# A hybrid encoder block on one core: projection r by token halves, with half of the features resident

## The chip, the cores and the metric

The kernel runs on one core of one Trainium2 chip. The metric is the device time of one execution in microseconds (us); it is given as the median of several runs. Engines are named as in the profile: PE (TensorE), DVE (VectorE), ACT (ScalarE), POOL (GpSimd) and SP (SyncE, from whose queue nearly all DMAs are issued).

## The reference

One layer, 1024 tokens of width 1024, all float32:

```
h = rmsnorm(x, norm_mix)
q, k, v, r, lr_f, lr_b, u, g_a, g_b = split(h @ w_in)      # 512,512,1024,1024,16,16,512,1024,1024
log_a = log_sigmoid(lr @ w_decay_up + b_decay) / 16        # forward and backward
o = gla_chunked(q, k, v, log_a_f, include_diag=True)       # 4 heads, keys 128, values 256
  + flip(gla_chunked(flip(q), flip(k), flip(v), flip(log_a_b), include_diag=False))
o = rmsnorm_per_head(o) * gla_norm * silu(r);  y_a = o @ w_branch_gla
y_b = (centred mean over windows 2/4/8/16 of u, minus u) @ w_pool_group * pool_scale
x = x + (sigmoid(g_a) * y_a + sigmoid(g_b) * y_b) @ w_out
gate, up = split(rmsnorm(x, norm_ffn) @ w_ffn_in);  x = x + (silu(gate) * up) @ w_ffn_out   # D_FF 2816
out = rmsnorm(x, norm_final)
```

## The kernel before

Every large matrix is split into a high and a low part (a cast on ACT, then a difference on POOL or DVE: `split_to`), and a product is three matmuls (`products`). Most of the large products are done by a Strassen scheme with seven block products p = 1 to 7, so sums of blocks are made on DVE and POOL beside the matmuls.

The order of the work is written out by hand; each engine runs its own queue in the order in which the program emits it, and the DMAs stand in SP's queue. What stands beside the matmuls is emitted by `pump(dt)`, which runs after each three matmuls (`mm3`) with dt = 1 for 512 columns. It keeps four lists:

- `put_off`: steps given by `soon(delay, step)`, first in, first out; `settle` empties the list.
- `pending`: splits of a weight set that `prepare` (called by `take`) has put there. The first comes out after 4 units, the second after 6, since `prepare` sets the credit to -2 and a split needs 2.
- `aside`: one generator of preparatory jobs (`prepare_beside`, `beside`). It counts down in every unit, but runs, at most one job a unit, only while `pending` is empty. `finish_beside` emits all that is left at once.
- `side`: generators begun by `begin`; each yields the units until its next step.

The stages, in order:

1. Norms, features `hT` (8 pairs of slots: pair kp and token half, each as `hh` and `hl`), values of head 0.
2. Low-rank decays, then `project_qk`: q and k of head 0 (four passes of 8 units, each a `feature_major`). Beside it `feature_jobs` makes the sums of features (`hs`) and their splits (`trh`, `trl`). The second half of feature pairs 0 and 1 is written to DRAM (`h_out`) and its slots are freed.
3. Gates: 16 units of Strassen products (u, q, k, v, the merge gates a and b). `Ahead.step` prepares unit weights four steps ahead (`wh`, `wl` from `fs` or `fraw`). `decays` runs as side work, and `pooling` after it. v is transposed and split by `Gates.turn`, which `finish_late` runs after the next product. In the last unit head 0 (`load_head`), the features' second half (`load_features`) and values are loaded.
4. r and attention: eight column tiles of r, for each both token halves with one weight set. `attention(h)` of the four heads runs as side work: a backward scan (7 steps), scores, a forward scan (8 steps) and a normalization, with `SCORES` and `STEP` units between steps. `load_head(h + 1)` and `load_values` fetch the next head. `gated` transposes a finished head and multiplies it by silu(r); `put_by` calls it at the end of each pass. Beside it run the sums of the branch and output weights (`branch_jobs`, `output_jobs`: tile `wsum`, written to `s_out` and `t_wo`), eight blocks of one load and four POOL operations, a job every 2 units.
5. Branch and output projections (`project`): 28 pieces of 8 units. `line_load`, `line_sums` and `line_make` prepare the pieces ahead of their use (`wraw`, `wh`, `wl`, and data as `dh`, `dl`); the tiles `wh` and `wl` have six buffers each, two for a piece.
6. FFN in and out, final norm.

All working tiles come from one pool of 39 slots of 4 KB a partition; a load whose slot isn't free waits in SP's queue. `take()` hands out a prepared weight set and calls `prepare` for the next, whose DMA is issued there.

Of the kernel before, what the change touches and what calls it, by code (L numbers as in the profile page):

```python
# [17 lines left out]
P = 128  # L18
# [33 lines left out]
def kernel(  # L52
# [159 lines left out]
    class Weights:  # L212
# [194 lines left out]
    qk_out = [[dram.tile([P, 2, HALF], F32, name=f"qk_out{h}{n}") for n in range(2)] for h in range(HEADS)]  # L407
    h_out = [[dram.tile([P, 2, HALF], F32, name=f"h_out{kp}{n}") for n in range(2)] for kp in range(2)]
    dec_out = [
# [201 lines left out]
    def decays():  # L611

        for h in range(HEADS):
            for half in (1, 0):
# [55 lines left out]
    def project_qk(amid):  # L670
        qk = [slot(s=s) for s in "qk"]
        for dst, scale in zip(qk, (DK**-0.5, 1.0)):
            w = take(dst is qk[0])
            for half in range(2):
                amid(dst is qk[1], half)
                ps = feature_major(w, hT, half)
                nc.scalar.activation(dst[:, half, :], ps[:, :], AF.Copy, scale=scale)
        for n, t in enumerate(qk):
            later(qk_out[0][n], t[:, :, :])

    def load_head(h):
        q, k = (slot(s=s) for s in "qk")
        qe, ke = {}, {}
        for t, src in ((k, qk_out[h][1]), (q, qk_out[h][0])):
            nc.sync.dma_start(t[:, :, :], src)
        for half in (1, 0):
            for n, (e, s) in enumerate(((qe, "qe"), (ke, "ke"))):
                e[half] = slot(s=s)
                nc.sync.dma_start(e[half][:, :, :], dec_out[h][half][n])
        heads[h] = q, k, qe, ke  # L690

# [11 lines left out]
    def apply_decay(h, half, d):  # L703
        q, k, qe, ke = heads[h]
        for eng, e, x_ in ((nc.vector, ke, k), (nc.gpsimd, qe, q)):
            eng.tensor_tensor(e[half][:, d, :], e[half][:, d, :], x_[:, half, :], op=ALU.mult)

# [3 lines left out]
    def attention(h):  # L711

        q, k, qe, ke = heads[h]

# [45 lines left out]
        if h == 0:  # L760
            for run in RUNS:
                apply_decay(0, *run)
                yield 1.5
            kt_of[0] = transposed_keys(0, 1, 1)
            yield 2
# [3 lines left out]
        for n in range(NT - 1, 0, -1):  # L769
# [9 lines left out]
            if n == 2:  # L779
                kts[0, 0] = transposed_keys(h, 0, 0)  # L780
                yield 0.5
        p = scores(0)
        yield SCORES
        o = [slot(shape=(4, DV), s="o") for _ in range(2)]
        ms = vec(NT, "oms")
        old = sf = None
        for n in range(NT):
            half, i = n // 4, n % 4
            op = bank(ps_g, "op")
            products(op[:, :DV], tokens(p, n), value(n), last=False)  # L790
            terms = []
            if n < NT - 1:
                terms.append((chunk_of(qe, n, 1), sb[half][:, i, :]))
            if n > 0:
                terms.append((chunk_of(qe, n, 0), sf[:, :]))
            for j, (a, b) in enumerate(terms):
                if j == len(terms) - 1 and n < NT - 1:
                    state, old = advance(old, n, 0, kts[half, 0])
                    sf = s1((DV,), "sf")
                    nc.scalar.activation(sf[:, :], state, AF.Copy, scale=factor(n + 1, 0, "before"))  # L800
                nc.tensor.matmul(op[:, :DV], a, b, start=False, stop=j == len(terms) - 1)  # L801
# [32 lines left out]

    STEP = 1.2

    def transposed_keys(h, half, d):
        ke = heads[h][3]
        kp = bank(ps_g, "kp")
# [123 lines left out]
    for half in range(2):  # L963
# [9 lines left out]
        nc.vector.tensor_tensor(lrT[64:96, half, :], ps[64:96, :], as_f32(lrT[64:96, half, :]), op=ALU.subtract)  # L973
    def first_unit(k, half):
        if k:
            gates_ahead.step()

    project_qk(first_unit)
    finish_beside()
# [47 lines left out]
    def line_make():  # L1027
        n = len(made)
        if n < len(line) and not (n // 2 == 1 and len(ob.get((1, 0), ())) <= n % 2):
# [53 lines left out]
    def branch_piece(p, c):  # L1083
# [10 lines left out]
        def make(raw):  # L1094
            b = {1: ob[0, 0], 2: ob[1, 0], 3: ob[1, 1], 4: ob[1, 0], 5: ob[0, 0], 6: t2s, 7: ob[0, 1]}[p][c]
            right = data_split(b)
# [92 lines left out]
    class Gates:  # L1189
# [12 lines left out]
        def run(self, p):  # L1202
# [71 lines left out]
    for n, run in enumerate(gate_runs):  # L1274
# [8 lines left out]
        for at, (of, p) in enumerate(run):  # L1283
# [33 lines left out]
    def project(base, products, collect, before, amid=None, first=FIRST, up=UP, pools_of=lambda p: U_BANKS if p == 1 else X_BANKS):  # L1317
        banks = {}
        for at, p in enumerate(products):
# [4 lines left out]
            for c in range(2):  # L1324
# [75 lines left out]
    def gated(j, half, sr):  # L1400

        tp = bank(ps_g, "tp")
        for i in range(4):
            nc.tensor.transpose(
                tp[:, i * P : (i + 1) * P],
                o_heads[j // 2][half][:, i, (j % 2) * P : (j % 2 + 1) * P], ident[:, :],
            )
        if j // 2 not in oT:
            oT[j // 2] = [slot(s="o") for _ in range(2)], []
        tiles, there = oT[j // 2]  # L1410
        nc.vector.scalar_tensor_tensor(
            tiles[half][:, j % 2, :], tp[:, :], g_gla[:, j : j + 1], sr, op0=ALU.mult, op1=ALU.mult
        )
        there.append((j, half))
        if len(there) == 4:
            c = j // 2 % 2
            for half, t in enumerate(tiles):
                if j < 4:
                    later(ob_out[0, half][:, 2 * c : 2 * c + 2, :], t[:, :, :])
                else:  # L1420
                    ob.setdefault((1, 1 - half), []).append(t)

    def put_by():
        if silu_r and silu_r[0][0] // 2 in o_heads:
            gated(*silu_r.pop(0))

# [8 lines left out]
    prepare_beside(chain(map(branch_jobs, range(4)), map(output_jobs, range(4))), 2)  # L1435
    for j in range(KT):
        w = take()
        r = slot(s="r")
        for half in range(2):
            ps = feature_major(w, hT, half)  # L1440
            flush()
            nc.scalar.activation(r[:, half, :], ps[:, :], AF.Silu)
            silu_r.append((j, half, r[:, half, :]))
# [465 lines left out]
```

## Time and profile before

| | us |
|---|---|
| runs | 1463.4, 1465.99, 1464.22 (median 1464.22) |
| the profiled execution | 1468.01 |
| its span, first to last instruction | 1466.3 |
| PE busy | 1381.7 (94%) |
| DVE busy | 886.8 (60%) |
| POOL busy | 768.9 (52%) |
| ACT busy | 647.4 (44%) |
| mean granted PE clock | 0.979 |

A wait row gives who waited, for what, the sum in us, the number of waits and the longest. A row of a group gives line, engine, operation, output<-inputs, shapes and count; then busy time in us, mean ns of one, and the idle time before them with what ended it. A row in order of time begins with its start and its duration in us; idle time of the engine before it, and what ended that, stands in brackets. SPq rows are DMA issues.

### The profile page before, as it was taken

Reading aid. Unit: us, or ns where it says so; the run is one execution under the profiler, and the core shown is the slowest. Engines: PE = TensorE matmul, PEld = TensorE weight load, DVE = VectorE, ACT = ScalarE, POOL = GpSimd, SP = SyncE. Lnnn points to the kernel's source line nnn. Section 1 sums busy time; section 2 is a strip of 40 time slices with the busy share of each in tenths; the row PEclk is TensorE's granted clock in tenths of the full one; section 3 lists DMA queues with packets and bytes.
Section 4 is the critical chain, followed back from the end, with each engine's and each line's share of the span. In section 5 each row is a group of like instructions: output and inputs, shape, how many; then the busy total and the mean of one; then the engine's idle time right before and its main releaser. Section 6 shows DMA issues by size and latency. Waiting matters only on the chain.

```text
span 1466.3 us, 18225 instructions
## 1 busy us (share of the span) xinstructions
PE 1381.7 (94%) x6365; PEld 1145.0 (78%) x6365; DVE 886.8 (60%) x1103; ACT 647.4 (44%) x1138; POOL 768.9 (52%) x576
## 2 busy tenths in 40 slices
PE   7979988999988989998898999999999999999997
PEld 7858767787877768877776888888888888888876
DVE  6876555687643766766867486555555555543353
ACT  6366765644533333444333643333333334353243
POOL 3244533455635453345764437666666668455354
PEclk9989999999999998999999999999999999999999
DMA  6334535566896786664622535545555556876452
GB/s 212 116 98 132 172 110 197 191 207 209 264 353 236 243 285 223 226 232 155 235 96 101 201 118 177 160 151 163 165 166 165 165 165 231 334 287 232 158 210 77
DMA packets 182588, 279.26 MB, mean 190 GB/s; under 512 B 12088, under 2 KB 102240, under 8 KB 182496
## 3 DMA queue, kind: packets, MB, share of 16 engines
q1 hardware_dynamic: 182496, 278.10, 55.8%
q8 instruction: 50, 0.82, 0.2%
q14 instruction: 42, 0.34, 0.1%
HBM read 182.37 MB, written 95.68 MB: 190 GB/s over the span
## 4 chain that ended last, share of the span: by engine, by line
PE 68%; DVE 9%; issue 7%; DMA 6%; POOL 5%; ACT 4%; SPq 0%; POOLq 0%; DVEq 0%; ACTq 0%
PE ps L269 62%; POOL wl L198 2%; DMA raw<-in_w_in_dram 2%; DMA fraw<-in_w_in_dram 1%; DVE hs L590 1%; DMA pl<-p_out 1%; PE op L801 1%; POOL wsum L590 1%; PE kv L269 1%; DMA hh<-h_out 1%; PE sc L748 1%; ACT wh L197 1%; PE yb L269 1%; DVE fs L866 1%; PE tr L316 1%
## 5 line engine op out<-in xcount | busy, mean ns | idle before, releaser
L198 POOL TENSOR_TENSOR wl<-fs,wh 128x512 fp32r<-128x512 f32 x144 | 198.1, 1378 | 205.6 <-ACT wh L197 173.6
L269 PE MATMUL ps<-gh,wh 128*128 128x512 f32 x616 | 240.6, 391 | 0.0
L269 PE MATMUL ps<-gh,wl 128*128 128x512 f32 x616 | 239.9, 390 | 0.0
L269 PE MATMUL ps<-gl,wh 128*128 128x512 f32 x616 | 239.9, 389 | 0.0
L198 POOL TENSOR_TENSOR wl<-fraw,wh 128x512 fp32r<-128x512 f32 x108 | 155.1, 1436 | 102.6 <-ACT wh L197 98.4
L198 POOL TENSOR_TENSOR ol<-gor,oh 128x1024 fp32r<-128x1024 f32 (+1 forms) x42 | 100.4, 2396 | 93.8 <-ACT oh L197 76.9
L269 PE MATMUL ps<-hh,wh 128*128 128x512 f32 x352 | 147.0, 417 | 0.0
L269 PE MATMUL ps<-hl,wh 128*128 128x512 f32 x352 | 139.3, 396 | 0.0
L269 PE MATMUL ps<-hh,wl 128*128 128x512 f32 x352 | 139.1, 395 | 0.0
L269 PEld LDWEIGHTS ps<-gh,wl 128*128 128x128 f32 x616 | 115.7, 188 | 23.9
L269 PEld LDWEIGHTS ps<-gl,wh 128*128 128x128 f32 x616 | 115.7, 188 | 23.8
L269 PEld LDWEIGHTS ps<-gh,wh 128*128 128x128 f32 x616 | 115.7, 188 | 23.7
L198 POOL TENSOR_TENSOR wl<-wraw,wh 128x512 fp32r<-128x512 f32 x56 | 91.2, 1655 | 75.3 <-ACT wh L197 75.3
L269 PE MATMUL ps<-oh,oh 128*128 128x512 f32 x308 | 120.1, 390 | 2.0 <-DVE x L1831 2.0
L269 PE MATMUL ps<-ol,oh 128*128 128x512 f32 x308 | 120.1, 390 | 0.8 <-DVE ol L198 0.8
L269 PE MATMUL ps<-oh,ol 128*128 128x512 f32 x308 | 119.9, 389 | 0.0
L269 PE MATMUL ps<-trh,wh 128*128 128x512 f32 x256 | 101.7, 397 | 10.6 <-ACT wh L197 8.9
L197 ACT CAST wh<-fs 128x512 fp32r<-128x512 f32 x144 | 88.3, 614 | 29.0 <-DVE fs L866 26.5
L269 PE MATMUL ps<-trh,wl 128*128 128x512 f32 x256 | 100.8, 394 | 0.2 <-POOL wl L198 0.2
L269 PE MATMUL ps<-trl,wh 128*128 128x512 f32 x256 | 100.7, 393 | 0.0
L198 DVE TENSOR_TENSOR ol<-wor,oh 128x1024 fp32r<-128x1024 f32 (+1 forms) x42 | 62.0, 1496 | 52.7 <-ACT oh L197 45.4
L198 POOL TENSOR_TENSOR wl<-raw,wh 128x512 fp32r<-128x512 f32 x23 | 31.4, 1379 | 98.3 <-ACT wh L197 98.3
(254 smaller groups left out, 3063.4 us busy)
## 6 DMA issues: line engine op xcount, KB each, us to landing
fraw<-in_w_ffn_in_dram SPq DMA_DIRECT2D x44, 512.0 KB, 6.0
gor<-g_out SPq DMA_DIRECT2D x35, 512.0 KB, 6.2
fraw<-in_w_in_dram SPq DMA_DIRECT2D x32, 512.0 KB, 6.7
g_out<-s SPq DMA_DIRECT2D x44, 256.0 KB, 2.4
wor<-t_out SPq DMA_DIRECT2D x20, 512.0 KB
g_out<-g SPq DMA_DIRECT2D x33, 256.0 KB, 2.3
x<-in_x_dram SPq DMA_DIRECT2D x16, 512.0 KB, 5.4
wor<-in_w_ffn_out_dram SPq DMA_DIRECT2D x15, 512.0 KB, 11.2
```

Source lines behind the costliest of these rows:

```text
L197: nc.scalar.copy(hi, src)
L198: eng.tensor_tensor(lo, src, as_f32(hi), op=ALU.subtract)
L269: nc.tensor.matmul(ps, a[i], b[j], start=first and n == 0, stop=last and n == 2, skip_group_check=onto)
L316: nc.tensor.transpose(ps[:, c], xt[:, k * P : (k + 1) * P], ident[:, :])
L590: op()
L748: nc.tensor.matmul(sc[d][:, i * CH : (i + 1) * CH], chunk_of(ke, n, d), chunk_of(qe, n, d), start=True, stop=True,)
L801: nc.tensor.matmul(op[:, :DV], a, b, start=False, stop=j == len(terms) - 1)
L866: nc.vector.tensor_tensor(s, a, b, op=op)
```

## The change

The first tile of r (column tile 0, both halves) is computed right after q and k of head 0, and written to `r_out`. The other seven tiles run in stage 4 with the token half as the outer loop, so their weights are loaded and split twice; only the first half of the features stays resident, all four pairs of the second half go to `h_out` and come back during the last two passes of the first half. The first two gate unit steps move from beside k to beside r's tile. `STEP` goes from 1.2 to 0.95, `SCORES` from 6 to 4.5, the pause after each round of decays from 10 to 6. The next head's k, q and values are loaded at other steps. `turn` is given to `soon` with a delay of 5. `finish_beside` in stage 4 stands after tile 5 of the second half, ahead of two more weight sets' use. In `project`, a second `line_make` runs when fewer than n + 3 pieces are made. `gated` keeps its tiles by head and half, and `put_by` takes the first entry whose head is ready.

```diff
-        + [(w_in, KT, R0 + j * P, P) for j in range(KT)]
+        + [(w_in, KT, R0 + j * P, P) for j in (0, *range(1, KT), *range(1, KT))]
...
-    for kp in range(2):
+    for kp in range(4):
         for n, part in enumerate(hT.pair(kp, 1)):
             later(h_out[kp][n], as_f32(part[:, :, :]))
...
-                yield 10
+                yield 6
...
-    SCORES = 6
+    SCORES = 4.5
...
+    def first_r():
+        w = take(False)
+        r = slot(s="r")
+        for half in range(2):
+            gates_ahead.step()
+            ps = feature_major(w, hT, half)
+            nc.scalar.activation(r[:, half, :], ps[:, :], AF.Silu)
+        later(r_out, r[:, :, :])
+
-    def load_features():
-        for kp in range(2):
+    def load_features(kps):
+        for kp in kps:
...
         p = scores(0)
+        if h + 1 < HEADS:
+            load_head(h + 1, "k")
         yield SCORES
...
-                if n == 2:
-                    load_head(h + 1)
+                if n == 1:
+                    load_head(h + 1, "q")
                 if n == 4:
                     load_values(h + 1, 1)
-                if 4 <= n < NT:
-                    apply_decay(h + 1, *RUNS[n - 4])
+                if n == 6:
+                    load_values(h + 1, 0)
+                if 3 <= n < 7:
+                    apply_decay(h + 1, "k", *RUNS[n - 3])
+                if 4 <= n:
+                    apply_decay(h + 1, "q", *RUNS[n - 4])
                 if n == NT - 1:
-                    load_values(h + 1, 0)
                     kt_of[h + 1] = transposed_keys(h + 1, 1, 1)
...
-    STEP = 1.2
+    STEP = 0.95
...
-    project_qk(first_unit)
+    project_qk()
+    first_r()
...
-                late.append(partial(self.turn, int(p == 7)))
+                soon(5, partial(self.turn, int(p == 7)))
...
             if last and at == 1:
                 fetch()
-                load_head(0)
-            elif last and at == 4:
-                load_features()
+                load_head(0, "k")
+            elif last and at == 3:
+                load_head(0, "q")
             elif last and at == 5:
                 prepare()
-            elif last and at == 6:
                 load_values(0, 1)
...
                 line_load()
                 line_make()
+                if len(made) < n + 3:
+                    line_make()
                 line_sums()
...
-    for j in range(KT):
-        w = take()
-        r = slot(s="r")
-        for half in range(2):
+    for half in range(2):
+        for j in range(1, KT):
+            w = take()
+            if j == 1 or j % 2 == 0:
+                r = slot(s="r")
+            if j == 1:
+                nc.sync.dma_start(r[:, 0, :], r_out[:, half, :])
+                silu_r.append((0, half, r[:, 0, :]))
             ps = feature_major(w, hT, half)
             flush()
...
-            if (j, half) == (KT - 2, 1):
+            if half == 0 and j >= KT - 2:
+                load_features((2 * j - 12, 2 * j - 11))
+            elif (j, half) == (KT - 3, 1):
                 finish_beside()
                 line_load()
                 line_load()
+            elif (j, half) == (KT - 2, 1):
                 load_block(0, 0)
+                line_make()
                 load_block(0, 1)
-            elif j == KT - 1:
+            elif (j, half) == (KT - 1, 1):
                 line_make()
```

More of the change, by code (lines that the diff above doesn't have):

```diff
@@ L407 @@
     qk_out = [[dram.tile([P, 2, HALF], F32, name=f"qk_out{h}{n}") for n in range(2)] for h in range(HEADS)]
-    h_out = [[dram.tile([P, 2, HALF], F32, name=f"h_out{kp}{n}") for n in range(2)] for kp in range(2)]
+    h_out = [[dram.tile([P, 2, HALF], F32, name=f"h_out{kp}{n}") for n in range(2)] for kp in range(4)]
+    r_out = dram.tile([P, 2, HALF], F32, name="r_out")
     dec_out = [
@@ L664, in decays, with project_qk @@
                         nc.sync.dma_start(dec_out[h][half][n][:, d, :], t[:, :])
-                yield 10
+                yield 6
     heads, v_heads, o_heads = {}, {}, {}
-    SCORES = 6
-    def project_qk(amid):
+    SCORES = 4.5
+    def project_qk():
         qk = [slot(s=s) for s in "qk"]
         for dst, scale in zip(qk, (DK**-0.5, 1.0)):
-            w = take(dst is qk[0])
+            w = take()
             for half in range(2):
-                amid(dst is qk[1], half)
                 ps = feature_major(w, hT, half)
@@ L679, in project_qk, with load_head @@
             later(qk_out[0][n], t[:, :, :])
[L681 to L685, printed above, removed]
+    def first_r():
[6 more added lines that the diff above has]
+        later(r_out, r[:, :, :])
+    def load_head(h, which):
+        me = heads.setdefault(h, {})
+        n = "qk".index(which)
+        whole = me[which] = slot(s=which)
+        me[which + "e"] = {}
+        nc.sync.dma_start(whole[:, :, :], qk_out[h][n])
         for half in (1, 0):
[L687 to L690, printed above, removed]
+            e = me[which + "e"][half] = slot(s=which + "e")
+            nc.sync.dma_start(e[:, :, :], dec_out[h][half][n])
     def load_values(h, half):
@@ L701, in load_features, with apply_decay @@
                 nc.sync.dma_start(as_f32(t[:, :, :]), h_out[kp][n])
[L703 to L706, printed above, removed]
+    def apply_decay(h, which, half, d):
+        eng = {"q": nc.gpsimd, "k": nc.vector}[which]
+        e = heads[h][which + "e"][half][:, d, :]
+        eng.tensor_tensor(e, e, heads[h][which][:, half, :], op=ALU.mult)
     RUNS = ((1, 1), (0, 1), (0, 0), (1, 0))
@@ L761, in attention @@
             for run in RUNS:
-                apply_decay(0, *run)
+                apply_decay(0, "k", *run)
+                apply_decay(0, "q", *run)
                 yield 1.5
@@ L1028, in line_make @@
         n = len(made)
-        if n < len(line) and not (n // 2 == 1 and len(ob.get((1, 0), ())) <= n % 2):
+        if n < len(line) and (n // 2 != 1 or n % 2 in ob.get((1, 0), ())):
             while len(loads) <= n:
@@ L1400, in gated @@
     def gated(j, half, sr):
+        h, i = j // 2, j % 2
         tp = bank(ps_g, "tp")
[L1403 to L1410, printed above, removed]
+        for t in range(4):
+            nc.tensor.transpose(tp[:, t * P : (t + 1) * P], o_heads[h][half][:, t, i * P : (i + 1) * P], ident[:, :])
+        tile_, there = oT.setdefault((h, half), (slot(s="o"), [])) if (h, half) not in oT else oT[h, half]
         nc.vector.scalar_tensor_tensor(
-            tiles[half][:, j % 2, :], tp[:, :], g_gla[:, j : j + 1], sr, op0=ALU.mult, op1=ALU.mult
+            tile_[:, i, :], tp[:, :], g_gla[:, j : j + 1], sr, op0=ALU.mult, op1=ALU.mult
         )
[L1414 to L1421, printed above, removed]
-    def put_by():
-        if silu_r and silu_r[0][0] // 2 in o_heads:
-            gated(*silu_r.pop(0))
+        there.append(j)
+        if len(there) == 2:
+            if h < 2:
+                later(ob_out[0, half][:, 2 * h : 2 * h + 2, :], tile_[:, :, :])
+            else:
+                ob.setdefault((1, 1 - half), {})[h - 2] = tile_
+    def put_by():
+        for n, (j, half, sr) in enumerate(silu_r):
+            if j // 2 in o_heads:
+                silu_r.pop(n)
+                gated(j, half, sr)
+                return
     def finish_heads():
@@ L1435 @@
     prepare_beside(chain(map(branch_jobs, range(4)), map(output_jobs, range(4))), 2)
[L1436 to L1439 removed]
+    for half in range(2):
+        for j in range(1, KT):
+            w = take()
+            if j == 1 or j % 2 == 0:
[3 more added lines that the diff above has]
+                silu_r.append((0, half, r[:, 0, :]))
             ps = feature_major(w, hT, half)
             flush()
[L1442 to L1443 removed]
+            nc.scalar.activation(r[:, j % 2, :], ps[:, :], AF.Silu)
+            silu_r.append((j, half, r[:, j % 2, :]))
             for _ in range(2):
                 put_by()
[L1446 removed]
+            if half == 0 and j >= KT - 2:
+                load_features((2 * j - 12, 2 * j - 11))
+            elif (j, half) == (KT - 3, 1):
                 finish_beside()
```

9 lines of the change are left out of this document (3 added, 6 removed).

## The prediction

> **What bounds the kernel now.** I read the page first, then the waits of TensorE, then TensorE in windows around each wait (start:end, length, busy and matmuls, mean granted clock, DMA share, GB/s), and last the queues of the stages that the diff touches.
>
> ```profile
> span 1466.3 us, 18225 instructions
> PE 1381.7 (94%) x6365; PEld 1145.0 (78%) x6365; DVE 886.8 (60%) x1103; ACT 647.4 (44%) x1138; POOL 768.9 (52%) x576
> ...
> PE ps L269 <- DVE dl L162: 12.9, 6, 3.7
> PE ps L269 <- ACT wh L197: 9.8, 2, 8.9
> PE vt L1241 <- DVE ga L1215: 7.2, 2, 5.1
> PE kv L269 <- ACT kt L197: 6.5, 2, 5.8
> PE tp L1404 <- DVE o L830: 5.3, 4, 2.6
> PE vt L1241 <- ACT ga L1222: 4.9, 2, 3.1
> PE op L801 <- ACT sf L800: 4.4, 5, 1.2
> ...
> 75.00:95.00 20.00, 10.92 (x38) 0.74 0.34 105
> 203.00:214.00 11.00, 5.93 (x25) 0.84 0.00 0
> 232.00:248.00 16.00, 12.12 (x62) 1.00 0.20 67
> 267.00:276.00 9.00, 5.87 (x23) 0.81 0.64 250
> 447.00:460.00 13.00, 7.21 (x25) 0.74 0.54 183
> 535.00:560.00 25.00, 16.25 (x67) 0.80 0.76 252
> 611.40:628.10 16.70, 16.70 (x105) 1.00 0.85 298
> 660.00:680.00 20.00, 15.60 (x60) 0.91 0.64 229
> 705.00:720.00 15.00, 11.22 (x35) 0.77 0.59 212
> 745.00:760.00 15.00, 11.56 (x50) 1.00 0.33 106
> 793.00:806.00 13.00, 8.11 (x29) 0.74 0.49 167
> ```
>
> TensorE is busy for 94% of the span, and the change leaves its matmuls as they are: r still takes 16 passes of 24. So time can only come from the 84.6 us in which it is idle (1466.3 - 1381.7) and from stretches at a lower clock, and it can only be lost by new waits. The waits name the places: feature sums (8.9, the ACT row), the turning of v (7.2 + 4.9), the start of attention (5.8), the gating of a finished head (5.3), the low halves `dl` in the two projections (12.9). The clock falls with most of them.
>
> **Unit of the steps.** The side work is paced in units of three 512-wide matmuls:
>
> ```profile
> 843.88 550.16 PE ps L269 x2427
> ```
>
> 550.16/2427 is 0.227 us a matmul, 0.68 us a unit, 5.44 us a pass of 8 units.
>
> **A. First r tile beside the feature sums.**
>
> ```profile
> 50.19 3.35 DVE L590 TENSOR_TENSOR hs<-hh,hl 128x1024 f32<-128x1024 f32 x2
> ...
> 85.03 1.23 DVE L575 TENSOR_TENSOR trl<-hs,trh 128x1024 fp32r<-128x1024 f32 x1 [0.56 <-ACT trh L584]
> 86.06 0.79 PE L269 MATMUL ps<-trh,wh 128*128 128x512 f32 x1 [8.91 <-ACT wh L197]
> 84.91 0.59 ACT L677 ACTIVATE k<-ps 128x512 f32<-128x512 f32 x1
> 451.46 1.28 ACT L1442 ACT_TABLE_LOAD   x1
> ```
>
> VectorE works without a pause from 50 to 86 us, and TensorE has nothing to do from 77.2 on. Two passes (10.9 us) now fall into that hole. The second needs the PSUM bank of k's first half (three banks in turn), copied out at 84.9; in the new order only three of the last four casts stand before that copy, so about 80.5: a wait of 1 us. The first gate unit's sums move behind the features on VectorE, to 86, so its second product starts near 89, as it does now (86.06 at half clock until 90.9). The extra writes of h (four of 512 KB) go into 50 to 66 us, where the DMA engines have room before r's weights are cast at 69. Silu brings a table load of 1.28 us here and one for Exp after it. Bounds: -11 (all hidden) to -6 (ScalarE late by both loads and a cast). I take -9.5, nearest to the hole's own row.
>
> **B. Gate stage.** Decays wait 6 units rather than 10 after each of 8 rounds: they end 32 units (22 us) earlier, at unit 212 rather than 244 of the stage. v's six turns fall at units 173 to 241, so the last three leave the decays' company, and with them the two waits for ScalarE's copies, 1.8 us (in window 232:248) and 3.1 us (267:276, with 0.19 x 9 = 1.7 of clock). "Five steps on" is one unit more than now (a product is four), 0.7 us for each of the other two waits. That is -8. Against it: the first rounds are denser on VectorE. -9 to +3; I take -6.
>
> **C. Start of attention.**
>
> ```profile
> 439.45 3.18 SPq L205 DMA_DIRECT2D raw<-in_w_in_dram  x2
> 449.95 0.62 ACT L197 CAST wh<-raw 128x512 fp32r<-128x512 f32 x1 [13.96 <-DMA raw<-in_w_in_dram]
> 442.01 0.39 PE L269 MATMUL ps<-hh,wh 128*128 128x512 f32 x1
> 440.00:450.00 10.00, 8.09 (x38) 6.38 (x36) 0.00 (x0) 0.05 (x1) 0.00 (x0) 1.00 1.05 390
> 549.64 1.00 SPq L205 DMA_DIRECT2D raw<-in_w_in_dram  x2
> 566.04 0.47 PE L269 MATMUL ps<-hh,wh 128*128 128x512 f32 x1
> ```
>
> The cast of r's second weights waits for its load and holds up the cast of the keys `kt` behind it on ScalarE. Without the h loads 2.1 MB leave the DMA queue (5.4 us at the 390 GB/s moved there), so the load lands near 444.5. But with halves outermost these weights are needed after one pass, at 442.0 (now the second half's first matmul), not two: TensorE waits until about 446.4, 4.4 us, where it now waits 5.8. Then kv follows without a wait, and the half clock (0.26 x 13 = 3.4) is shorter. +4 to -6, I take -2.5.
>
> **D. Middle of attention.** The next head's loads go out some 7 units earlier, so the waits for vh and o at 535:560 (8.75 idle there, up to 5 of clock) shrink. Steps shortened by 0.25 unit take 0.17 us of cover from each of 56: 9.5 us if every step waited, but now only 5 forward steps wait, 4.4 us in all. Four pairs of forward steps fall into one unit, about 1 us each. Fourteen more weight splits lie on POOL and ScalarE beside matmuls. The second half of the features comes back through 8 loads (4.2 MB) around units 48 to 58; the last four can be a few us late. -10 to +8; I take -2.
>
> **E. End of r: the new wait.** The branch and output sums (`beside`, 56 jobs) run only in units where no weight split is pending. A weight set pends for 6 units after `take`. Before, that left 10 or 11 of 16 units, enough for a job every 2 units. Now it leaves 3 of every 8: 12 passes give 36 jobs by unit 96, where `finish_beside` puts the other 20 at once: 12 POOL sums with their loads and stores, and only then, on the same SP queue, two `wraw` loads and the weights of the last pass.
>
> ```profile
> L590 POOL TENSOR_TENSOR wsum<-wsum 128x512 f32<-128x512 f32 x16 | 21.2, 1331 | 3.8 <-DMA wsum<-in_w_out_dram 3.4
> L198 POOL TENSOR_TENSOR wl<-raw,wh 128x512 fp32r<-128x512 f32 x14 | 18.0, 1297 | 63.4 <-ACT wh L197 63.4
> L301 POOL TENSOR_TENSOR ors<-ors,half_neg 128x8 f32<-128x8 f32 x4 | 6.7, 1672 | 4.7 <-DVE ors L300 4.6
> 501.43 2.19 DVE L830 TENSOR_SCALAR o<-o,ors 128x256 f32<-128x256 f32 x8 [1.55 <-POOL ors L301]
> 591.18 19.05 SPq L571 DMA_DIRECT2D t_wo<-wsum  x6
> SPq L571 <- POOL wsum L590: 70.7, 24, 15.4
> ```
>
> The SP row shows that the queue does stand still for these sums, 19 us over six stores. Issue to landing, `wsum` first, then `raw` (min/median/max):
>
> ```profile
> DMA to landing us min/median/max: 2.4/4.2/7.5
> DMA to landing us min/median/max: 2.8/4.7/10.5
> ```
>
> From the end of the split at unit 94 (1.9 us after TensorE gets there): four sums 5.3, the next block's load 0.4 + 4.2, two sums 2.7, the last block's load 0.4 + 4.2, four sums 5.3: 22.5. Stores, `wraw`, `raw` issued: 2.5. `raw` lands: 4.7 (10.5). Cast and split 1.9. Then `ors`, in POOL's queue behind that split, 1.7, and the eight scalings 2.2, which the transposes ahead of the last pass wait for: 35.5 to 41.3, with the 1.9 some 37.4 to 43. TensorE is there after 10 units (6.8) and what window 611.4:628.1 holds besides its 8 units (16.7 - 5.4 = 11.3, six steps and the scores) and a gating, 1: 19. Stall 18 to 24, and 1.7 to 3.4 of low clock after it. If the weights come in time it is 0. I take +22.
>
> **F. Projections.** `line_make` now stays three pieces ahead rather than two, and head 3 is gated before the branch begins. The waits at 660:680 (4.4 idle), 705:720 (3.8), 745:760 (3.4) and 793:806 (4.9) are each for a piece made one piece before its use, its low half queued on VectorE behind the last product's collection. A piece of 5.44 us earlier it stands before that collection. With clock (1.8, 3.4, 0, up to 3.4) this is 16.5 to 25. What could be late next is VectorE itself, and the `wh` buffers (six, all taken by three pieces). 0 to -23; I take -17.
>
> The clock is a two-state one here: 8.91 idle us brought 10.2 at half, and the window 535:560 shows 0.80 though no single wait in it was over 2.6. The Trainium skill ("TensorE: Matmul & The Clock Gate", Part 1) says that the clock halves after at least one idle window of about 3.4 us; by that alone 535:560 would have lost no clock and D would be -1 instead of -2. The trace disagrees, since several short waits were enough.
>
> **Sum.** -9.5 - 6 - 2.5 - 2 + 22 - 17 = -15. The profiled execution took 1468.0 us (span 1466.3 and 1.7 around it), 3.8 over the median; so 1453.0 for it, and on the median 1464.2 - 15 = 1449.2.
>
> **Rivals.** (1) The wait of E doesn't come, since SP runs far enough ahead: -37, 1427. For it: SP issued r's seventh weights at 549.6 (row in C), 16 us before TensorE began the pass ahead of which they are taken, at 566.0. Against: the stores need POOL, which needs casts paced by TensorE. (2) Slower: every pass waits for its own weights. One pass is 5.4 us plus its steps, and load, cast and two splits take 0.4 + 4.7 + 0.6 + 2.6 = 8.3, or 14 with the longest landing. Where the pass holds few steps (the pass beside each head's scores, four) TensorE would wait 3.5 and lose 1.7 of clock: 4 x 5.2 = 21, making +6, 1470. It decides from landings over about 7 us. For it: 10.5 at 439; against: POOL is idle 63 us before these splits. (3) The projections are bound by VectorE, F gives nothing: +2, 1466, no change.
>
> **Chances.** Forecast 0.52 (own range 1438 to 1460), rivals 0.14, 0.22 and 0.12. The bound of no change is 0.2%, 2.9 us. Faster 0.66 (forecast and first rival), same 0.11 (the third), slower 0.23 (the second, and a little of the third). The range reaches from the first rival to the second.
>
> **What would show it.** A: TensorE without the wait at 77. B: fewer `vt` waits. C: a `ps` wait for `wh` or `wl` near 442 in place of kv's. E: `wsum` sums bunched at the end of r, and one wait of about 20 us for `o` or r's `wh` some 10 us of matmuls before the branch; its absence makes the forecast wrong by that much. F: `dl` waits below 4 us in all.

## The result, and the profile after

The changed kernel takes 1450.45 us (median of four runs, 1448.66 to 1452.15) beside 1464.39 for the kernel before on the same chip: a ratio of 0.9904, 95% interval [0.9886, 0.9921], 14 us faster. Its profiled execution took 1448.66 us (span 1446.6), 1.8 under its median, where that of before (1468.01) was 3.6 over its own. So the two traces lie 19.4 us apart (19.7 us in span), 5.4 more than the medians.

First the page and the waits of TensorE (total, times, longest):

```profile
span 1446.6 us, 18339 instructions
PE 1369.8 (95%) x6365; PEld 1137.3 (79%) x6365; DVE 895.6 (62%) x1103; ACT 658.1 (45%) x1154; POOL 792.3 (55%) x590
...
PE tp L1417 <- DVE o L844: 25.1, 6, 21.2
PE op L812 <- ACT sf L811: 5.8, 5, 1.8
PE ps L269 <- ACT ga L1220: 3.8, 2, 2.0
PE ps L269 <- ACT wh L197: 3.5, 2, 1.8
PE vt L1252 <- ACT ga L1233: 2.9, 2, 2.2
PE kv L269 <- ACT kt L197: 2.2, 3, 1.4
PE ps L269 <- ACT k L677: 1.8, 1, 1.8
PE ps L269 <- DVE dl L162: 0.7, 1, 0.7
```

The large waits of before have shrunk: the feature sums' wait for `wh` (8.9) is gone, v's wait for VectorE (7.2) too, `kt` went from 6.5 to 2.2, `dl` from 12.9 to 0.7. Small ones have grown or are new: `op` for `sf` went from 4.4 to 5.8, and products' waits for `ga` on ScalarE went from 0.8 to 3.8. In the stead of the large ones stands a wait that was not there, 21.2 us for `o`; the other five for `o` make 3.9. TensorE in windows (start:end, length, busy and matmuls, clock, DMA share, GB/s): the feature sums, the start of attention, the first head's gating, the second half's middle, the end of r, the branch and output projections:

```profile
70.00:95.00 25.00, 22.51 (x98) 1.00 0.32 106
432.00:450.00 18.00, 15.60 (x65) 0.91 0.82 258
485.00:500.00 15.00, 12.23 (x60) 0.89 0.40 147
535.00:560.00 25.00, 24.53 (x152) 1.00 0.66 233
605.00:642.00 37.00, 14.24 (x57) 0.68 0.91 321
644.00:803.00 159.00, 157.03 (x708) 1.00 0.52 175
```

The projections hold 2 us of idle time in 159 and run at full clock. The end of r holds 22.8 us of idle time in 37. There the timeline, by queue (start, duration, engine, operation, in brackets the idle time before it and what ended it):

```profile
614.26 1.26 POOL L591 TENSOR_TENSOR wsum<-wsum 128x512 f32<-128x512 f32 x1 [2.28 <-DMA wsum<-in_w_out_dram]
618.28 1.26 POOL L591 TENSOR_TENSOR wsum<-wsum 128x512 f32<-128x512 f32 x1
627.87 1.26 POOL L198 TENSOR_TENSOR wl<-raw,wh 128x512 fp32r<-128x512 f32 x1 [8.34 <-ACT wh L197]
629.09 1.64 POOL L301 TENSOR_TENSOR ors<-ors,half_neg 128x8 f32<-128x8 f32 x1
...
610.68 9.20 SPq L572 DMA_DIRECT2D t_wo<-wsum  x6
619.94 0.98 SPq L1049 DMA_DIRECT2D wraw<-in_w_branch_gla_dram  x2
621.01 0.96 SPq L205 DMA_DIRECT2D raw<-in_w_in_dram  x2
...
627.18 0.62 ACT L197 CAST wh<-raw 128x512 fp32r<-128x512 f32 x1 [18.64 <-DMA raw<-in_w_in_dram]
...
630.76 3.88 DVE L844 TENSOR_SCALAR o<-o,ors 128x256 f32<-128x256 f32 x3 [21.46 <-POOL ors L301]
...
632.16 0.48 PE L1417 MATMUL tp<-ident,o 128*128 128x128 f32 x1 [21.17 <-DVE o L844]
```

Read it from the bottom up. TensorE waits for the scaled `o`, that for `ors` on POOL, which stands in POOL's queue behind the low half of r's last weights; that waits for ScalarE's cast, the cast for a load, and the load was issued at 621.0, behind six stores on SP that waited for the bunched sums.

### The profile page after: what moved, and what is told of

It is laid out like the page before. It is cut to its first block, busy times and chain, and to the rows that moved or that the text cites. A ratio compares the mean times of both kernels' runs of the same rounds, so it can differ in the third digit from the quotient of the medians.

```text
span 1446.6 us, 18339 instructions
## 1 busy us (share of the span) xinstructions
PE 1369.8 (95%) x6365; PEld 1137.3 (79%) x6365; DVE 895.6 (62%) x1103; ACT 658.1 (45%) x1154; POOL 792.3 (55%) x590
## 4 chain that ended last, share of the span: by engine, by line
PE 73%; DVE 10%; issue 5%; DMA 4%; ACT 3%; POOL 3%; SPq 0%; POOLq 0%; DVEq 0%; ACTq 0%
PE ps L269 67%; DMA raw<-in_w_in_dram 1%; POOL wl L198 1%; PE op L812 1%; POOL wsum L591 1%; DVE o L844 1%; PE yb L269 1%; DVE so L748 1%; DVE ws L1009 1%; DVE hs L591 1%; DVE res L1819 1%; DMA wsum<-in_w_out_dram 1%; PE sc L756 1%; ACT wh L197 1%; PE kv L269 1%
## 5 line engine op out<-in xcount | busy, mean ns | idle before, releaser
L198 POOL TENSOR_TENSOR wl<-raw,wh 128x512 fp32r<-128x512 f32 x37 | 50.4, 1366 | 135.5 <-ACT wh L197 135.5
L198 POOL TENSOR_TENSOR wl<-wraw,wh 128x512 fp32r<-128x512 f32 x56 | 95.0, 1724 | 41.9 <-ACT wh L197 41.8
```

Of the source, the lines that this page charges most:

```text
L198: eng.tensor_tensor(lo, src, as_f32(hi), op=ALU.subtract)
```

## The experiments

The theory: E's wait costs some 26 us and is made by the bunch of sums; F and the smaller parts pay for it. The rivals: the bunch isn't the cause (another holder of the queues), the gain in the projections comes from the earlier gating and not from the look-ahead, and the first r tile's matmuls are not free. Each ratio is to the kernel before on the same chip.

**1. The sums spread out.** The sums may run while a weight split is pending (`free[0]` is set where stage 4 begins), so that fewer are left for the end.

```diff
-            if aside[0][1] <= 0 and not pending:
+            if aside[0][1] <= 0 and (not pending or free[0]):
```

> Changed kernel, but the preparatory sums of stage 4 may run while a weight split is pending (one job every 2 units, as paced before). By units, 48 of 56 jobs are out at unit 96 instead of 36, so finish_beside finds 8 instead of 20. Theory (the bunch of sums on POOL and SP makes the wait at the end of r): the wait for o of 21.2 us falls to under 6 us and most of the half clock behind it goes, 23 us less than the changed kernel, about 1427 us. Rival (the wait comes from r's halves outermost, the last weights being asked for only one pass ahead): the wait stays near 20 us and the time near 1450. Third possibility: sums between the splits hold up casts in the middle of attention, which gives back up to 10 us.

1448.58 us, 0.9884 [0.9863, 0.9905]: not to be told apart from the changed kernel. The wait for `o` is halved, and the timeline shows why no more than that, and what was paid for it (a wait in the middle of attention that the changed kernel hasn't):

```profile
633.42 0.48 PE L1418 MATMUL tp<-ident,o 128*128 128x128 f32 x1 [10.59 <-DVE o L845]
...
610.37 9.89 SPq L573 DMA_DIRECT2D t_wo<-wsum  x6
620.31 0.98 SPq L1050 DMA_DIRECT2D wraw<-in_w_branch_gla_dram  x2
621.39 0.96 SPq L206 DMA_DIRECT2D raw<-in_w_in_dram  x2
...
457.03 0.50 PE L270 MATMUL ps<-hh,wl 128*128 128x512 f32 x1 [2.41 <-POOL wl L199]
```

The bunch is smaller (seven sums from 607 to 620 instead of fourteen from 596), but the load of r's last weights still leaves at 621.4, since it stands behind the stores of the last two blocks. SP is a holder of its own: the expectation took POOL and SP for one cause, which would go with the bunch. TensorE also begins to wait 11.8 us later, at 622.8 and not 611.0: 5 of these it had lost by the first `kv`, the others went in attention, where the 2.41 us wait above is for a split.

**2. The sums finished one pass later.**

```diff
             elif (j, half) == (KT - 3, 1):
-                finish_beside()
...
             elif (j, half) == (KT - 2, 1):
+                finish_beside()
```

> Changed kernel with finish_beside alone moved one pass later, behind the request for the last weights of r. Theory: the last weights and the normalization no longer stand behind the bunch, so the wait for o before the last pass falls under 4 us; but the remaining 17 jobs (some 10 POOL sums of 1.3 us and two loads of 4 to 5 us) are still emitted together ahead of the weight splits of the first branch pieces, so 10 to 18 us of waiting move to the first pieces of the branch: 1436 to 1446 us. Rival (only the order of the last weights behind the sums matters): nothing new waits, about 1427 us.

1450.08 us, 0.9903 [0.9877, 0.9929]: the mechanism is the theory's, but the time is above its range, and nothing is gained. r's last weights are early, the longest wait for `o` is 2.4, and the same time turns up one step on, at the branch's first piece, whose loads are now the ones behind the stores:

```profile
PE ps L269 <- ACT wh L197: 18.6, 3, 14.9
PE tp L1417 <- DVE o L844: 7.4, 7, 2.4
```

So it is the bunch, and not its place, that costs the time.

**3 and 4. The look-ahead.** Once taken out of the changed kernel, once put alone into the kernel before:

```diff
                 line_make()
-                if len(made) < n + 3:
-                    line_make()
```

> Changed kernel without the second line_make in project. By the prediction's part F the waits for dl come back: +17 us (1467), of which those at the start of the branch stay away since head 3 is gated before it. Span from the first branch piece to the first FFN product: 158.6 us in the changed kernel, 183.2 before; 172 to 178 expected here. Rival (the gain of the projections comes from the earlier gating alone, since pieces 2 and 3 can then be made in time): under +6 us.

1451.89 us, 0.9914 [0.9895, 0.9933]: no change, as the rival of that expectation has it. In the changed kernel the two lines do nothing: in the traces with and without them, each engine has the same instructions in the same order. The reason stands in the first lines of `line_make`, here as the kernel before has them:

```python
        n = len(made)
        if n < len(line) and not (n // 2 == 1 and len(ob.get((1, 0), ())) <= n % 2):
```

Both kernels make two pieces during r and then one beside each piece, which keeps three ahead as long as no call is skipped. The kernel before gates head 3 in the branch, so beside the second piece `ob[1, 0]` lacks head 3, the call makes nothing, and from there on the look-ahead is two. The changed kernel has gated head 3 by then and skips nothing. So its look-ahead of three comes from the earlier gating and not from these lines. What the depth is worth this run can't tell. In the kernel before, with the two lines added:

> Kernel before with the second line_make alone. By part F the waits behind collections go (705:720, 745:760, 793:806: 12 us idle and about 5 of clock), those at 660:680 stay, since head 3 is gated in the branch: 1446 to 1452 us. Rival (gating early is what the look-ahead needs): 1458 to 1464 us.

1447.57 us, 0.9884 [0.9867, 0.9901]: 16.4 us from these two lines alone, which here make up for the skipped piece. From the branch's first product to the next stage it is 167.1 us instead of 183.2. One `dl` wait of any size stays, near the start, where the kernel before gates head 3:

```profile
PE ps L269 <- DVE dl L162: 5.1, 2, 4.4
```

**8. The look-ahead held at two pieces** in the changed kernel, with head 3 gated as early as there:

```diff
-                line_make()
-                if len(made) < n + 3:
+                if len(made) < n + 2:
                     line_make()
```

> Changed kernel with the look-ahead in project held at two pieces (a piece is made only while fewer than n + 2 are there). The run without the second line_make left that depth as it was, since the earlier gating keeps three pieces made from the start. Theory F (the depth is what removes the dl waits): first branch piece to first FFN product goes from 158.6 to 172 to 178 us, 1464 to 1470 in all. Rival (early gating and the sums done by then are enough): under +5 us.

1471.23 us, 1.0047 [1.0029, 1.0065]: 21 us slower than the changed kernel, and slower than before. The waits for `dl` are back, with the clock (0.95 over the projections, as before):

```profile
PE ps L269 <- DVE dl L162: 11.1, 5, 3.4
...
648.30:828.40 180.10, 165.96 (x707) 0.95 0.44 153
```

180.1 us here beside 158.7. So the depth carries F, and early gating without the depth is worth little. Taken with 3 and 4: early gating is what gives the changed kernel its depth, and in the kernel before the two lines can give it too.

**5. r's last weights asked for ahead of the sums.**

```diff
             elif (j, half) == (KT - 3, 1):
+                fetch()
                 finish_beside()
```

> Changed kernel, the load of r's last weights asked for just ahead of finish_beside (one fetch moved); nothing else. In the run with the sums spread, POOL was through with them at 620 and the wait for o went on to 634, behind a load that SP issued at 621.4 after the last store. Theory now (two queues in a row: SP holds the load behind the stores, POOL holds the split behind the sums): the SP part goes, the POOL part stays. POOL ends its sums at 619.5 in the changed kernel and TensorE is there at 611.0, so split 1.3, ors 1.6, scalings 2.2 end near 625: the wait falls from 21.2 to 12 to 15 us, and the time by 7 to 10, to about 1441. Rival (POOL alone holds it up): wait 19 to 21, 1449. Rival (SP alone): under 4 us, 1428.

1438.52 us, 0.9825 [0.981, 0.984], 12 us better than the changed kernel for one line. What is left of the wait is POOL's part:

```profile
620.70 1.26 POOL L591 TENSOR_TENSOR wsum<-wsum 128x512 f32<-128x512 f32 x1
621.91 1.26 POOL L198 TENSOR_TENSOR wl<-raw,wh 128x512 fp32r<-128x512 f32 x1
623.13 1.64 POOL L301 TENSOR_TENSOR ors<-ors,half_neg 128x8 f32<-128x8 f32 x1
...
610.57 1.13 ACT L197 CAST wh<-raw 128x512 fp32r<-128x512 f32 x2
...
626.20 2.11 PE L1417 MATMUL tp<-ident,o 128*128 128x128 f32 x8 [13.04 <-DVE o L844]
```

The cast is done at 611.7, and its split starts at 621.9, without idle time before it, when the last sum has left POOL. With SP's part taken away the wait is 8 us shorter, and 13 are left, which are POOL's; the time is somewhat better than the 1441 expected.

**6 and 12. Both together,** the early load with the sums spread over all of r (the edits of 5 and 1), and the early load with the sums spread over r's second half only (`free[0] = half == 1`).

> Changed kernel with the sums spread over pending units (the first experiment) and the last weights' load asked for ahead of finish_beside. Both queues are eased: theory gives a wait for o of at most 4 us at the end of r, no long half clock, and 1430 to 1436 us; the attention keeps the waits of the spread run (some 4 us more than in the changed kernel). If the end still shows 10 us of waiting, a third cause holds it.

> Changed kernel with the last weights asked for ahead of finish_beside, and sums allowed beside pending splits in the second half of r alone. The run that spread them throughout lost some 7 us in the middle of attention, from the third pass on. Theory (the price of spreading is paid where the attention's chain waits on ScalarE and POOL, early passes above all): end wait for o under 4 us as there, the middle as in the changed kernel up to the seventh pass: 1429 to 1434 us. Rival (the price is paid anywhere): 1437.

1437.02 us, 0.9818 [0.9803, 0.9832], and 1436.42, 0.9799 [0.9782, 0.9816]. The wait at the end of r falls to 2.45 in both, 10.6 less than in experiment 5, and yet neither can be told apart from it; both are slower than the theories had them, and 12 is where its rival put it. The branch starts at 632.2 and 632.3, after 635.1 there. From the first `kv` to the start of the wait for `o` attention takes 169.5 and 169.1 us, 7 more than the 162.3 of experiment 5. In 6 half of that is idle time (17.5 us beside 13.9), with a wait of 3.24 for `wl` at 453 and four for `o` at about 500 (4.5 in all, beside 2.3 in three); the rest is half clock, 6.8 us beside none. In 12 the idle time grows by only 1 us, and 10.2 us stand at half clock. So spreading the sums was paid for in both. That attention's steps wait for POOL behind the sums is shown for the one wait for `wl`; how much of the half clock comes from the sums is not shown.

**7. The sums carried on in the branch,** finished ahead of its product 7 (the fifth in order) rather than at the end of r.

```diff
+        if p == 7:
+            finish_beside()
...
-                finish_beside()
```

> Changed kernel without finish_beside at the end of r: the output sums go on, a job every 2 units, beside the branch products, and are finished ahead of its fifth product. Theory: the wait of 21 us goes, and POOL has room in the branch (two splits of 1.3 to 1.7 in 5.44 us a piece) for one more sum in 2 units only just; 1426 to 1432 us. Rival (POOL becomes the bound of the branch): waits for wl of 5 to 10 us appear there, 1434 to 1440.

1447.83 us, 0.989 [0.9873, 0.9906]: both the theory's range and the rival's are missed. r does end without the wait (the branch starts at 625.8, not 644.0), but the projections take 173.3 us instead of 158.7:

```profile
648.63 0.80 PE L269 MATMUL ps<-dh,wh 128*128 128x512 f32 x1 [5.29 <-ACT wh L197]
...
640.96 2.56 SPq L572 DMA_DIRECT2D t_wo<-wsum  x2
643.62 0.38 SPq L1049 DMA_DIRECT2D wraw<-in_w_branch_gla_dram  x1
...
644.00:672.00 28.00, 20.91 (x67) 0.82 0.85 307
```

The stores take their place in SP's queue with them, and now it is the branch's weights that stand behind: this load is issued at 643.6, after two stores that waited for their sums, and four more stores hold SP for 7.4 us ahead of the next one.

**9. The first r tile's matmuls left out.** Its 48 matmuls beside the feature sums are not issued, and the features are put through Silu in their place; r's first 128 columns are not computed.

```diff
-            ps = feature_major(w, hT, half)
-            nc.scalar.activation(r[:, half, :], ps[:, :], AF.Silu)
+            for k in range(KT):
+                pump(1)
+            nc.scalar.activation(r[:, half, :], as_f32(hT(0, 0)[0]), AF.Silu)
```

> Changed kernel with the 48 matmuls of r's first tile left out (its silu is taken of features instead, so r's first 128 columns are not computed); its weights, table load, slot, store and the pacing of the side work stay. Theory A (the two passes run in a hole that the feature sums on VectorE leave): the hole comes back, and leaving out 10.9 us of matmuls saves only 1 to 3.5 us; the gate stage's second product starts at 88 to 90 us instead of 90.8. Rival (they cost their full time, and the gain of the change has other sources): 9 to 11 us less, about 1440.

1449.42 us, 0.9896 [0.9881, 0.991]: 10.9 us of matmuls less, and no gain that can be seen. The hole of before comes back, deeper, and with it the half clock:

```profile
70.00:95.00 25.00, 12.01 (x39) 0.66 0.32 105
...
86.90 0.80 PE L269 MATMUL ps<-hh,wh 128*128 128x512 f32 x1 [12.82 <-ACT wh L197]
```

So the rival falls: the two passes cost next to nothing where the change puts them. Whether that is nothing or the 1 to 3.5 us that theory A expected the intervals can't tell. The second gate product did not come at 88 to 90 us, as expected, but at 93.2, since the matmuls ahead of it run at half clock.

**10. The gate stage as before** in the changed kernel (`yield 10` for the decays, v turned through `late` instead of `soon(5, ...)`).

> Changed kernel with part B undone: 10 units after each round of decays, and turn after the next product. Theory B: the waits for ga before the transposes of v come back (now 2.9 us in two, 12.1 before), +6 us, about 1456, the first pass of r starting 5 to 7 us later. Rival (the gate stage's gain came from the feature stage's new order): no change of more than 2 us.

1455.56 us, 0.994 [0.9927, 0.9952]: 5 us slower than the changed kernel, as theory B has it; the two edits were not tried one by one. The waits of v that the change removed are back:

```profile
PE vt L1252 <- DVE ga L1226: 5.8, 2, 4.6
PE vt L1252 <- ACT ga L1233: 5.1, 2, 3.3
```

**11. Tiles outermost again in r:** the seven tiles use one weight set for both halves, as before. With the loop three things go back to their old places: of the features' second half only two pairs of four are written out and read back, `finish_beside` stands after tile 6's second half, and the first piece of the branch is made in the last tile. The rest of the change is kept.

```diff
-    for half in range(2):
-        for j in range(1, KT):
-            w = take()
+    for j in range(1, KT):
+        w = take()
...
+        for half in range(2):
             ps = feature_major(w, hT, half)
```

> Changed kernel with r's other seven tiles in the old loop order (tile outermost, one weight set for both halves, second half of features 0 and 1 loaded back at the end of the gates as before); first tile, shorter steps, head loads and look-ahead as changed. Units: seven weight sets leave 10 of 16 units for the sums, so none is left to be bunched. Theory (the wait at the end of r comes from weights loaded twice): the 21 us wait goes, the start of attention is 3 to 5 us worse than in the changed kernel, 1426 to 1433 us. Rival (slots: with 16 slots of features the next head's loads wait, and attention loses what the end gains): 1440 to 1450.

1431.16 us, 0.9769 [0.9751, 0.9786]: the fastest of all, 19 us below the changed kernel and 34 below before. TensorE goes through the end of r without a pause. The expectation had no sums left to be bunched; the trace has ten on POOL in a row all the same, from 593 to 609 (fourteen in the changed kernel), and six stores stand in SP's queue as long as ever. But nothing that TensorE needs stands behind them. One weight set serves two passes, so the last set is asked for at 575, some 33 us ahead of its first pass, and its splits leave POOL by 593.0, ahead of the bunch:

```profile
575.28 2.69 SPq L205 DMA_DIRECT2D raw<-in_w_in_dram  x2
599.63 9.82 SPq L572 DMA_DIRECT2D t_wo<-wsum  x6
...
600.00:632.00 32.00, 32.00 (x175) 1.00 0.91 336
...
PE kv L269 <- ACT kt L197: 7.9, 4, 2.9
...
PE 1375.0 (96%) x6365; PEld 1142.3 (80%) x6365; DVE 891.8 (62%) x1103; ACT 651.5 (46%) x1140; POOL 775.9 (54%) x576
```

It does not get back all of E's 26 us: the attention before it, taken without that wait, is about 9.5 us longer (from the first `kv` to the branch 178.5 us, beside 195.4 - 26.4 = 169.0). That is the clock. The idle time in it is about the same, 13.6 us beside 12.8 up to the wait in the changed kernel, but four half-clock stretches lie in it, 23.0 us, after the waits for `kt` among others, and one of 3.4 in the changed kernel's; half of the difference is 9.8 us. Whether the loop order makes them, or the sums that now run there, this run doesn't separate: with halves outermost and the sums spread, experiments 6 and 12 have 181.0 and 180.4 us. Of the orders tried, tiles outermost with the rest of the change is the fastest.

## Why the prediction was right, and where it was not

The forecast, 1449.2, came to within 1.3 us of the median, by its own mechanism: all parts moved in the direction given, the new wait came where it was put, and E and F, the two large terms, were confirmed one by one, F though not in where it comes from. That the total fits better than the terms is partly luck: E was taken 4 us too small and F 7.5 us too small, which cancel in part, and between the traces it is 19.7 us and not 15. In the marks of the two traces:

| part | predicted | measured |
| --- | --- | --- |
| A, first r tile | -9.5 | -8.6 |
| B, gate stage | -6 | -6.2 (-3.8 by the middle of ten other executions) |
| C, start of attention | -2.5 | -4.2 |
| D, middle of attention | -2 | about -2.7 |
| E, end of r | +22 | about +26 |
| F, projections | -17 | -24.5 |
| sum | -15 | -19.7 (medians: -14) |

**A** was right. The wait at 77 is gone; one of 1.84 us for the bank of `k`, foreseen as 1, came:

```profile
81.20 0.50 PE L269 MATMUL ps<-hh,wh 128*128 128x512 f32 x1 [1.84 <-ACT k L677]
```

The second gate product begins at 90.8, not at about 89. Before, its start at 86.1 with 4.8 us at half clock was worth one at 88.5; so 2.3 of the 10.9 us are lost, about as much as the wait above and one of 0.66 for a split at 88. Experiment 9 shows that the two passes do run in the hole.

**B** was right in mechanism and size. From the second gate product to the last `yb` it is 341.6 us after 347.8. In the ten other profiled executions with the same gate stage (experiments 1 to 3, 5 to 9, 11 and 12) that stretch was 341.9 to 346.2, in the middle about 344, so the profiled execution was some 2 us better than usual there, which is part of what the traces differ by more than the medians. Experiment 10 puts the part at 5. v's waits fell from 12.1 to 2.9; the products' waits for `ga`, 3.8 after 0.8, were not foreseen.

**C** was named rightly: `kv` follows almost without a wait and the wait went to r's weights. It was 1.78 us, and 0.62 for the low half, where 4.4 was expected: the load was issued at 434.3 already, and the matmuls went on at 440.05, not at 446.4.

**D** can only be had as a rest: from the first `kv` to the branch it is 195.4 us after 185.4, with two passes (10.9) fewer. With the 2.8 us that the half clock cost after `kv` before, and which count under C, this is D + E = 10.9 + 10.0 + 2.8 = +23.7. Less E's 26.4 that leaves -2.7.

**E** was right in its chain, link by link, and a little small in size. The wait was 21.17, inside 18 to 24, and two of 0.79 followed; with 3.6 for the clock (23.9 us at half, of which 7.3 after the matmuls resumed) that is 26.4. The prediction's own terms add up to 19.7 to 27.4, and the +22 that it took lies low in them; the clock alone is a little above its 1.7 to 3.4. What the prediction did not say is how the chain divides: it added SP's and POOL's parts into one sum, and experiments 1 and 5 show two holders. Taking one away leaves the other, 10.6 or 13.0 us.

**F** is where the prediction missed, in the size and in where the depth comes from. It counted 16.5 to 25 us in the four waits and then took 17, keeping a share back in case VectorE or the `wh` buffers would be late next. Neither was. Before, the projections held 16.5 us of idle time and ran at a clock of 0.95; now 2 us of idle time are left in 159, at full clock:

```profile
639.00:822.00 183.00, 166.49 (x713) 0.95 0.43 150
```

Three pieces ahead is what brings this, as predicted: experiment 8 shows 21 us for the third piece. But the prediction gave the third piece to the new lines in `project`, and experiment 3 shows that in the changed kernel they add none; the earlier gating, named there as a second thing, makes it. That the two came in one change hid the error. In the kernel before the lines do make it, 16.4 us in experiment 4; the 4.4 us wait left there, with 6.8 us of half clock beside it, is what late gating still costs.

**The rivals.** The first (no wait at the end of r) and the third (nothing from F) fell with E and F. The second, each pass waiting for its weights, did not come: r's `wh` waits are 1.8 and 1.7 us, the second outside r's passes. Experiments 6, 11 and 12 show that the first would have been worth 13 to 19 us and not E's whole 22, since attention gets longer as the wait goes, in good part by half clock.

What stays open: the few us by which the gate stage differs from one execution to the next, which of the moved loads sets D, and what sets off the half-clock stretches in attention that take back part of what experiments 6, 11 and 12 gain.

## What to carry to other kernels

Work that is "beside" in idle units is only beside as long as there are such units: when a loop is turned round, count the units again in which its side work may run, and where the rest of it will be put down in one piece. In an issue queue that is served in order, a store that waits for a computation holds every load behind it; put the load ahead of such a store first (12 us here, one line); spreading the computation as well gave nothing more that could be told apart. A piece made one step earlier than the collection that used to delay it is worth the sum of its waits with their clock; keep none of it back unless a row shows what would be late next. And where two edits could bring the same gain, ask which of them acts: here the lines written to look further ahead did nothing once an earlier step no longer made a call skip.

## What was not expected of the hardware

The clock can halve among small gaps. In the window 485:500 of the changed kernel no wait was over 1.01 us, and a stretch of 3.4 us at half clock lay in it:

```profile
491.19 0.33 PE L1417 MATMUL tp<-ident,o 128*128 128x128 f32 x1 [0.88 <-DVE o L844]
492.53 1.59 PE L1417 MATMUL tp<-ident,o 128*128 128x128 f32 x6 [1.01 <-DVE o L844]
```

It needn't: in experiment 5 the same three waits (0.45, 0.88 and 1.01 us, from 492 to 495) pass at full clock, as does all of this stretch:

```profile
448.00:560.00 112.00, 100.44 (x594) 1.00 0.81 287
```

All half-clock stretches of these traces, but for the last in each, which runs to the end, last a multiple of about 3.41 us (3.41, 6.83 and 23.89 in the changed kernel, 10.24 before). The Trainium skill ("TensorE: Matmul & The Clock Gate", Part 1) has the clock halve after at least one idle window of about 3.4 us. The wait at the end of r agrees, with 23.9 us at half clock around 21.2 of idle time; the window 485:500 (0.89) does not, as the single waits in it are far shorter. The same part tells, under a second failure mode, of a kernel whose short idle times between groups of matmuls made the clock swing, and with that the window agrees; how much short idle time it takes, no run here shows.

And a Silu set ahead of the Exp steps costs nothing that can be seen. The kernel of experiment 11 has two instructions on ScalarE more than before (1140 after 1138), as many as the two table loads, 1.28 us each, at 86.7 and 94.3 in the changed kernel. TensorE's two waits at that place, the 1.84 us above and the 0.66 for a split on POOL, hang on a copy and a cast that end ahead of the first of them, and it waits for nothing from there to 130 us.
